# Norms that take their power on a few columns, and low parts of weights made on VectorE, in a hybrid decoder step

## The chip, the cores and the metric

One Trainium2 chip, one core of it. The metric is the device time of one execution in microseconds. Engines in the rows: PE is TensorE (PEld its weight loads), DVE is VectorE, ACT is ScalarE, POOL is GpSimd, SP is the queue that issues the DMAs.

## What is computed

One layer of a decoder trunk for 2048 new positions of a prompt and 64 tokens of running sequences (8 x 8), all in fp32, 1024 columns wide. Half of the mixer is a diagonal state space model (S5), half a gated linear recurrence (HGRN2). Cut to what matters here:

```python
def rmsnorm(x, g):
    r = x * lax.rsqrt(jnp.mean(x * x, axis=-1, keepdims=True) + EPS)
    return r * g

h = rmsnorm(x, norm_mix)
proj = h @ w_in                        # 1024 -> 512 + 4 * 512
y5 = s5_mixer(...)                     # scan, gelu, GLU
yh = hgrn2_mixer(...)                  # chunked recurrence
x = x + jnp.concatenate([y5, yh], -1) @ w_out
h2 = rmsnorm(x, norm_ffn)
x = x + (jax.nn.silu(h2 @ w_gate) * (h2 @ w_up)) @ w_down   # 1024 -> 2816 -> 1024
y = rmsnorm(x, norm_final)
```

## The kernel before

Tokens lie in the free dimension: the 2112 tokens are three blocks of 704 (FT), each two halves of 352 (FH), and the features lie on the 128 partitions. The norms before the FFN and at the end therefore sum over partitions.

**Products.** Every fp32 product is made of three matmuls in the fp32r type: the operand is split into a high part (ScalarE's copy, hi) and a low part (the difference, lo), and hi·hi, hi·lo and lo·hi are added. The output projection, gate and up, and down run by a seven-product scheme for 2 x 2 blocks of the matrices: `w_prep` loads the four quarters of a weight tile into a raw tile (`wr`, two buffers), makes four sums and differences of them on VectorE (L1037, L1038, L1044, L1045), and splits seven operands: ScalarE writes the high part (L1031), GpSimd the low part (L1032). Operands rotate over 7, later 10 buffers (`e.ws`). `x_slots` does the same for the activations, whose low part is VectorE's (L1009).

**A unit.** `seven` interleaves two weight tiles: for each of seven products and each tile 12 matmuls of 352 columns (`nk` = 4, in one group of three `nk` = 3), a set, and after each set a `sink`. Products use three kinds of PSUM bank in the order A Q B A B A A; a later set adds into a bank that an earlier one has left, so it waits for the earlier sink. Sinks are VectorE's sums from PSUM (`acc_sink` L1091, `gate_sink` L1105, `up_sink` L1128) or ScalarE's copies. In gate and up, VectorE also makes the product (L1129, L1119) and four combinations for the down projection (L976 to L979).

**Stages.** First the mixer's own projections and scans, then `mix` for the three blocks (output projection with `w_out`), `combine_y` (combinations of the mixer's output, through DRAM) and `norm2` (the norm before the FFN, its combinations stored to `h_s`); then `ffn` for the three blocks: 11 gate and up units, then for three groups of columns two units of the down projection. `final` of a block is issued after two units of the next block's `ffn`, the last one at the end.

**A norm.** `norm_r` squares on ScalarE, adds up eight tiles on VectorE (`sum`, L1169), sums over partitions with an fp32 matmul by a matrix of ones (L1174), which leaves the same row of 352 sums on all 128 partitions, scales on VectorE (L1175) and takes the power −0.5 on GpSimd for 128 x 704 elements (L1176). VectorE multiplies with the result (`rr_f` in `norm2` at L1185, `rr_z` in `final` at L1201). The norm at the start works otherwise: `inv_rms` (L285) takes the power on a few columns of row sums, `spread` (L293) puts them on a diagonal and spreads it by matmuls.

**Order.** A scheduler sets each engine's order by modelled times; every engine runs its queue in order. Tiles come from pools, a new one waits for the old one's readers.

Of the kernel before, what the change touches and what calls it, by code (L numbers as in the profile page):

```python
# [9 lines left out]
F32 = mybir.dt.float32  # L10
F32R = mybir.dt.float32r
I32 = mybir.dt.int32
AF = mybir.ActivationFunctionType
ALU = mybir.AluOpType
# [4 lines left out]
P = 128  # L19
D = 1024  # L20
# [8 lines left out]
EPS = 1e-6  # L29
# [236 lines left out]
def tiles_of(t0, n):  # L266
    r = []
    while n > 0:
        w = min(P, n)
        r.append((t0, w))  # L270
        t0 += w
        n -= w
    return r


def parts_of(tiles):
    nt = len(tiles)
    full = sum(1 for t in tiles if t[1] == P)
    parts = [(P, 0, full)] if full else []
    if full < nt:  # L280
        parts.append((tiles[-1][1], full, nt))
    return parts


def inv_rms(e, ss, tiles, r, name):  # L285
    nc = e.nc
    st = e.small.tile([P, 4], F32, tag="st", name=f"st_{name}")
    for rows, a, b in parts_of(tiles):
        nc.vector.tensor_scalar(st[:rows, a:b], ss[:rows, a:b], 1.0 / D, EPS, op0=ALU.mult, op1=ALU.add)
        nc.gpsimd.tensor_tensor(r[:rows, a:b], st[:rows, a:b], e.mhalf[:rows, 0:b - a], op=ALU.pow)  # L290


def spread(e, r, tiles, name):  # L293
    nc = e.nc
    dg = e.diag.tile([P, 4, P], F32, tag="dg", name=f"dg_{name}")
    for rows, a, b in parts_of(tiles):
        nc.vector.tensor_tensor(dg[:rows, a:b], e.ident[:rows, None, :].to_broadcast([rows, b - a, P]),
                                r[:rows, a:b, None].to_broadcast([rows, b - a, P]), op=ALU.mult)
    pr = e.ps_x.tile([P, 512], F32, tag="x", name=f"rr_{name}")
    for j, (o, w) in enumerate(tiles):  # L300
        nc.tensor.matmul(pr[:, o:o + w], e.ones[:w], dg[:w, j, :w], start=True, stop=True)
    return pr
# [25 lines left out]
def op_norm(e, t0, n, r, name):  # L328
    nc = e.nc
    pr = spread(e, r, tiles_of(0, n), name)  # L330
    pcs = pieces_of(n)
    op = []
    for j, (k, nk) in enumerate(pcs):
        flat = raw_tile(e, f"x{name}_{j}")[:, :nk * n]
        raw = flat.rearrange("p (k t) -> p k t", t=n)
        nc.sync.dma_start(raw, fm(e.i["xT"], k, nk, t0, n))
        for i in range(nk):
            nc.vector.scalar_tensor_tensor(raw[:, i], raw[:, i], e.gain[:, k + i:k + i + 1], pr[:, :n],
                                           op0=ALU.mult, op1=ALU.mult)
        hi, lo = wtile(e, f"x{name}_{j}", e.ops)  # L340
        split(e, flat, hi[:, :nk * n], lo[:, :nk * n], nc.gpsimd if j % 2 else nc.vector)
        op.append((hi, lo))
    return (t0, n, op_k(op, pcs, n))
# [608 lines left out]
FT = 704  # L952
FH = FT // 2
# [60 lines left out]
def w_prep(e, mats, nk):  # L1014

    nc = e.nc
    n = nk * P
    v = nc.vector
    out = [[] for _ in mats]
    gens = []  # L1020

    def prep(srcs, name, ops):
        raw = e.wraw.tile([P, 6, 512], F32, tag="wr", name=f"wr_{name}")
        for fh in range(2):
            nc.sync.dma_start(raw[:, 2 * fh:2 * fh + 2, :n], srcs[fh].rearrange("p (h f) -> p h f", h=2))
        a11, a12, a21, a22, s1, s2 = (raw[:, i, :n] for i in range(6))

        def sp(src):
            ws = e.ws.pick()
            hi, lo = (ws.tile([P, 512], F32R, tag="w" + c, name=f"w{c}_{name}_{len(ops)}")[:, :n] for c in "hl")  # L1030
            nc.scalar.activation(hi, src, AF.Copy)  # L1031
            nc.gpsimd.tensor_tensor(lo, src, hi.bitcast(F32), op=ALU.subtract)  # L1032
            ops.append((hi, lo))

        sp(a11)
        yield
        v.tensor_tensor(s1, a21, a22, op=ALU.add)  # L1037
        v.tensor_tensor(s2, s1, a11, op=ALU.subtract)  # L1038
        sp(a12)
        yield  # L1040
        sp(s1)
        yield
        sp(s2)
        v.tensor_tensor(a12, a12, s2, op=ALU.subtract)  # L1044
        v.tensor_tensor(a21, a11, a21, op=ALU.subtract)  # L1045
        yield
        sp(a12)
        yield
        sp(a21)
        yield  # L1050
        sp(a22)
        yield

    gens = [prep(srcs, name, ops) for (srcs, name), ops in zip(mats, out)]
    for _ in range(7):
        for g in gens:
            next(g)
    return out
# [98 lines left out]
def norm_r(e, x, name):  # L1157

    nc = e.nc
    tot = None  # L1160
    for j in range(4):
        for d in (j, j + 4):
            if tot is None:
                tot = e.nrm.tile([P, FT], F32, tag="sum", name=f"sum_{name}", bufs=1)
                nc.scalar.activation(tot, x[d], AF.Square)
                continue
            sq = e.nrm.tile([P, FT], F32, tag="sq", name=f"sq_{name}_{d}")
            nc.scalar.activation(sq, x[d], AF.Square)
            nc.vector.tensor_tensor(tot, tot, sq, op=ALU.add)  # L1169
    r = e.nrm.tile([P, FT], F32, tag="sq", name=f"rr_{name}")  # L1170
    for h in range(2):
        hs = slice(h * FH, h * FH + FH)
        ps = e.psN.tile([P, 512], F32, tag="n", name=f"ss_{name}_{h}")[:, :FH]
        nc.tensor.matmul(ps, e.ones, tot[:, hs], start=True, stop=True)  # L1174
        nc.vector.tensor_scalar(r[:, hs], ps, 1.0 / D, EPS, op0=ALU.mult, op1=ALU.add)  # L1175
    nc.gpsimd.tensor_tensor(r, r, e.mhalf[:, 0:1].to_broadcast([P, FT]), op=ALU.pow)  # L1176
    return r


def norm2(e, b, x):  # L1180
    nc = e.nc
    r = norm_r(e, x, f"f{b}")
    for j in range(4):
        for d in (j, j + 4):
            nc.vector.scalar_tensor_tensor(x[d], x[d], e.gain[:, KD + d:KD + d + 1], r, op0=ALU.mult, op1=ALU.mult)  # L1185
        B = [x[d][:, h * FH:h * FH + FH] for d in (j, j + 4) for h in range(2)]
        T = e.mtmp.tile([P, 4, FH], F32, tag="mt", name=f"ht{b}_{j}")
        combine(nc.vector, [T[:, i] for i in range(4)], *B)
        dst = e.h_s[b]
        for slot, t in ((0, B[0]), (1, B[2]), (4, B[3])):  # L1190
            nc.sync.dma_start(dst[:, slot, j], t)
        nc.sync.dma_start(dst[:, 2:4, j], T[:, 0:2])
        nc.sync.dma_start(dst[:, 5:7, j], T[:, 2:4])


def final(e, b, x):
    nc = e.nc
    r = norm_r(e, x, f"z{b}")
    for j in range(4):
        for d in (j, j + 4):  # L1200
            nc.vector.scalar_tensor_tensor(x[d], x[d], e.gain[:, 2 * KD + d:2 * KD + d + 1], r, op0=ALU.mult, op1=ALU.mult)  # L1201
            nc.sync.dma_start(e.o["yT"][d * P:(d + 1) * P, b * FT:(b + 1) * FT], x[d])
# [253 lines left out]
```

## Time and profile before

| what | value |
|---|---|
| median of 3 runs | 3372.87 us (3363.42 to 3374.15) |
| the profiled execution | 3370.24 us, span 3368.5 us |
| mean granted TensorE clock | 0.861 of full |
| GpSimd, six powers of a norm (L1176) | 338.0 + 337.9 us |
| GpSimd, low parts of weights (L1032) | 354.9 + 382.7 + 353.0 + 143.1 us, 798 instructions |

The rows that were read stand further below. In a row of a group, the line number is that of the kernel before; then engine, operation, output<-inputs by the program's names, shape and count; after the bar the busy time in us and the mean of one in ns, then idle time of the engine just before such instructions and what ended most of it. In a timeline, the number in brackets is the idle time before the instruction and what released it. PEclk is the granted TensorE clock as a share of 2.4 GHz.

### The profile page before, as it was taken

What the parts mean: (1) busy time and instruction counts of PE and PEld (TensorE: products, weight loads), DVE (VectorE), ACT (ScalarE), POOL (GpSimd) and SP (SyncE); (2) the same over time, 40 slices, a digit from 0 to 9 for tenths busy, and PEclk for the clock granted to TensorE, in tenths of its full rate; (3) what the DMA queues carried; (4) which work ended last, traced back from release to release, by engine and by line L of the source; (5) the groups of instructions that cost most, each with busy time, mean ns of one, the idle gap of its engine ahead of it and who ended that gap; (6) DMA issues with size and microseconds to landing.
All of it is one profiled execution on the core that took longest, in us unless ns stands there. A gap on an engine that the chain in (4) does not pass through costs nothing.

```text
span 3368.5 us, 44865 instructions
## 1 busy us (share of the span) xinstructions
PE 2398.2 (71%) x16813; PEld 2210.8 (66%) x16813; DVE 2269.8 (67%) x2692; ACT 996.7 (30%) x1848; POOL 2300.7 (68%) x1587
## 2 busy tenths in 40 slices
PE   7989999997713705029999985298998816898840
PEld 6977677785703705029998985288988816898840
DVE  8754545455596896946678788667777795667730
ACT  4322222222301302004434442043434402344310
POOL 4176585511587698866667778976767797666778
PEclk9999999998856857559999998599999957999975
DMA  8865644545414704123324431142353204334300
GB/s 253 226 226 163 182 152 144 161 141 194 162 59 149 258 16 143 57 83 125 138 100 159 142 138 47 68 166 104 138 176 131 99 4 167 114 118 156 131 19 34
DMA packets 249323, 441.57 MB, mean 131 GB/s; under 512 B 80265, under 2 KB 165586, under 8 KB 249106
## 3 DMA queue, kind: packets, MB, share of 16 engines
q1 hardware_dynamic: 249106, 438.71, 39.1%
q8 instruction: 132, 2.16, 0.3%
q14 instruction: 85, 0.70, 0.1%
HBM read 314.86 MB, written 123.76 MB: 130 GB/s over the span
## 4 chain that ended last, share of the span: by engine, by line
PE 30%; DVE 21%; POOL 19%; DMA 12%; issue 10%; POOLq 3%; ACT 2%; SPq 1%; DVEq 0%; ACTq 0%
POOL rr_f L1176 7%; PE pA_u L1076 4%; POOLq L1448 3%; POOL rr_z L1176 3%; PE pA_g L1076 3%; DMA wr_u<-in_w_up_u 3%; PE pA_d L1076 3%; DVE ct L976 2%; DMA wr_wd<-in_w_down_u 2%; POOL wl_wd L1032 2%; PE ps_v L263 2%; PE ps_u L263 2%; DVE s L1129 2%; PE ps_f L263 1%; PE pQ_g L1076 1%
## 5 line engine op out<-in xcount | busy, mean ns | idle before, releaser
L1032 POOL TENSOR_TENSOR wl_u<-wr_u,wh_u 128x512 fp32r<-128x512 f32 x231 | 354.9, 1541 | 198.5 <-ACT wh_u L1031 154.6
L1032 POOL TENSOR_TENSOR wl_wd<-wr_wd,wh_wd 128x512 fp32r<-128x512 f32 (+1 forms) x252 | 382.7, 1545 | 151.9 <-ACT wh_wd L1031 137.8
L1032 POOL TENSOR_TENSOR wl_g<-wr_g,wh_g 128x512 fp32r<-128x512 f32 x231 | 353.0, 1531 | 140.4 <-ACT wh_g L1031 136.2
L1176 POOL TENSOR_TENSOR rr_z<-rr_z,mhalf 128x704 f32<-128x704 f32 x3 | 338.0, 112665 | 18.5 <-DVE rr_z L1175 18.5
L1176 POOL TENSOR_TENSOR rr_f<-rr_f,mhalf 128x704 f32<-128x704 f32 x3 | 337.9, 112625 | 10.9 <-DVE rr_f L1175 10.9
L1076 PE MATMUL pA_g<-xh_h,wh_g 128*128 128x352 f32 x528 | 186.1, 352 | 220.5 <-ACT s L1103 137.2
L1076 PEld LDWEIGHTS pA_g<-xh_h,wh_g 128*128 128x128 f32 x528 | 107.1, 203 | 231.7 <-ACT s L1103 138.1
L1076 PE MATMUL pA_g<-xh_h,wl_g 128*128 128x352 f32 x528 | 182.1, 345 | 98.8 <-POOL wl_g L1032 98.8
L1076 PE MATMUL pA_o<-xh_y,wh_wo 128*128 128x352 f32 x192 | 73.2, 385 | 247.3 <-ACT xh_y L1008 117.3
L1076 PE MATMUL pA_u<-xh_h,wh_u 128*128 128x352 f32 x528 | 178.7, 338 | 85.3 <-ACT u L1126 72.7
L1032 POOL TENSOR_TENSOR wl_wo<-wr_wo,wh_wo 128x512 fp32r<-128x512 f32 x84 | 143.1, 1731 | 109.2 <-ACT wh_wo L1031 100.2
L1076 PE MATMUL pA_d<-xh_s,wh_wd 128*128 128x352 f32 x528 | 179.7, 340 | 44.3 <-DVE acc_d L1091 44.1
L1076 PEld LDWEIGHTS pA_o<-xh_y,wh_wo 128*128 128x128 f32 x192 | 43.3, 227 | 254.3 <-ACT xh_y L1008 118.9
L1031 ACT ACTIVATE wh_wd<-wr_wd 128x512 fp32r<-128x512 f32 (+1 forms) x252 | 140.5, 588 | 221.7 <-DMA wr_wd<-in_w_down_u 97.7
L1129 DVE TENSOR_TENSOR s<-s,u 128x352 f32<-128x352 f32 x99 | 183.0, 1849 | 11.9 <-ACT s L1106 6.1
L1031 ACT ACTIVATE wh_g<-wr_g 128x512 fp32r<-128x512 f32 x231 | 143.1, 624 | 150.9 <-DMA wr_g<-in_w_gate_u 69.8
L1031 ACT ACTIVATE wh_u<-wr_u 128x512 fp32r<-128x512 f32 x231 | 143.0, 625 | 149.7 <-DMA wr_u<-in_w_up_u 47.7
L1076 PE MATMUL pA_g<-xl_h,wh_g 128*128 128x352 f32 x528 | 180.5, 342 | 0.0
L1106 ACT ACTIVATE s<-s 128x352 f32<-128x352 f32 x99 | 49.2, 497 | 431.7 <-DVE s L1105 430.9
L1076 PE MATMUL pA_d<-xh_s,wl_wd 128*128 128x352 f32 x528 | 176.1, 334 | 0.0
L1076 PE MATMUL pA_d<-xl_s,wh_wd 128*128 128x352 f32 x528 | 176.0, 333 | 0.0
L1076 PE MATMUL pA_u<-xh_h,wl_u 128*128 128x352 f32 x528 | 175.2, 332 | 0.5 <-POOL wl_u L1032 0.5
(495 smaller groups left out, 8546.6 us busy)
## 6 DMA issues: line engine op xcount, KB each, us to landing
wr_g<-in_w_gate_u SPq DMA_DIRECT2D x66, 512.0 KB, 4.5
wr_u<-in_w_up_u SPq DMA_DIRECT2D x66, 512.0 KB, 5.8
xr_s<-s_s SPq DMA_DIRECT2D x42, 704.0 KB, 4.3
wr_wd<-in_w_down_u SPq DMA_DIRECT2D x48, 512.0 KB, 5.7
s_s<-T SPq DMA_DIRECT2D x132, 176.0 KB, 1.8
s_s<-s SPq DMA_DIRECT2D x99, 176.0 KB, 1.9
xr_h<-h_s SPq DMA_DIRECT2D x21, 704.0 KB, 4.4
wr_wo<-in_w_out_u SPq DMA_DIRECT2D x24, 512.0 KB, 7.2
```

What stands on the lines that cost most here:

```text
L263: e.nc.tensor.matmul(out, whl[k][a], xhl[k][b], start=start and i == 0, stop=stop and i == len(seq) - 1)
L976: v.tensor_tensor(t[0], b12, b11, op=ALU.subtract)
L1031: nc.scalar.activation(hi, src, AF.Copy)
L1032: nc.gpsimd.tensor_tensor(lo, src, hi.bitcast(F32), op=ALU.subtract)
L1076: nc.tensor.matmul(ps, W[i][w][:, ks], X[i][x][:, k], start=first and k == 0 and c == 0, stop=i in (1, 4, 6) and k == nk - 1 and c == 2, s ...
L1106: nc.scalar.activation(s[w], s[w], AF.Silu)
L1129: v.tensor_tensor(s[w], s[w], u[w], op=ALU.mult)
L1176: nc.gpsimd.tensor_tensor(r, r, e.mhalf[:, 0:1].to_broadcast([P, FT]), op=ALU.pow)
L1448: with tile.TileContext(nc, schedule_with_timeline_sim=True) as tc:
```

## The change

`norm_r` transposes its sums. For each half the sums over partitions come from three matmuls with the sum tile as the stationary operand and one column of ones as the moving one: 352 tokens land on the partitions of three columns (128, 128 and 96 rows). `inv_rms` scales them on VectorE and takes the power on GpSimd, two instructions (128x2 and 96x1) each. A new function, cut out of `spread`, multiplies the identity with them to a diagonal; three matmuls by ones spread it over the partitions; ScalarE copies the result to the tile `r`. All PSUM tiles of this come from the pool `psN` with one buffer. In `w_prep` the low part goes from GpSimd to VectorE. Lines after the new function move by 6, after `norm_r` by 13.

```diff
-def spread(e, r, tiles, name):
+def diagonal(e, r, tiles, name):
     nc = e.nc
     dg = e.diag.tile([P, 4, P], F32, tag="dg", name=f"dg_{name}")
     for rows, a, b in parts_of(tiles):
         nc.vector.tensor_tensor(dg[:rows, a:b], e.ident[:rows, None, :].to_broadcast([rows, b - a, P]),
                                 r[:rows, a:b, None].to_broadcast([rows, b - a, P]), op=ALU.mult)
+    return dg
+
+
+def spread(e, r, tiles, name):
+    nc = e.nc
+    dg = diagonal(e, r, tiles, name)
     pr = e.ps_x.tile([P, 512], F32, tag="x", name=f"rr_{name}")
...
             nc.scalar.activation(hi, src, AF.Copy)
-            nc.gpsimd.tensor_tensor(lo, src, hi.bitcast(F32), op=ALU.subtract)
+            v.tensor_tensor(lo, src, hi.bitcast(F32), op=ALU.subtract)
...
     for h in range(2):
-        hs = slice(h * FH, h * FH + FH)
-        ps = e.psN.tile([P, 512], F32, tag="n", name=f"ss_{name}_{h}")[:, :FH]
-        nc.tensor.matmul(ps, e.ones, tot[:, hs], start=True, stop=True)
-        nc.vector.tensor_scalar(r[:, hs], ps, 1.0 / D, EPS, op0=ALU.mult, op1=ALU.add)
-    nc.gpsimd.tensor_tensor(r, r, e.mhalf[:, 0:1].to_broadcast([P, FT]), op=ALU.pow)
+        o = h * FH
+        tl = tiles_of(0, FH)
+        ss = e.psN.tile([P, 512], F32, tag="n", name=f"ss_{name}_{h}")
+        for j, (c, w) in enumerate(tl):
+            nc.tensor.matmul(ss[:w, j:j + 1], tot[:, o + c:o + c + w], e.ones[:, 0:1], start=True, stop=True)
+        rc = e.small.tile([P, 4], F32, tag="r", name=f"r_{name}_{h}")
+        inv_rms(e, ss, tl, rc, f"{name}_{h}")
+        dg = diagonal(e, rc, tl, f"{name}_{h}")
+        pr = e.psN.tile([P, 512], F32, tag="n", name=f"pr_{name}_{h}")
+        for j, (c, w) in enumerate(tl):
+            nc.tensor.matmul(pr[:, c:c + w], e.ones[:w], dg[:w, j, :w], start=True, stop=True)
+        nc.scalar.activation(r[:, o:o + FH], pr[:, :FH], AF.Copy)
     return r
```

The order that the scheduler makes is the same on all engines up to the first unit of the output projection. Behind it, VectorE's queue in a gate and up unit of the first block (`s_8`, `u_8` and `T_8` are the running unit's tiles, `wr_g`, `wr_u` the next one's raw tiles) reads, before the change:

```order
L1038 TENSOR_TENSOR wr_u_0_13075<-wr_u_0_13075 128x512
L1045 TENSOR_TENSOR wr_u_0_13075<-wr_u_0_13075 128x512
L1105 TENSOR_TENSOR s_8_0_12954<-s_8_0_12954,pB_g_0_12912 128x352
L1044 TENSOR_TENSOR wr_g_0_13068<-wr_g_0_13068 128x512
L1128 TENSOR_TENSOR u_8_0_12968<-u_8_0_12968,pB_u_0_12927 128x352
L1044 TENSOR_TENSOR wr_u_0_13075<-wr_u_0_13075 128x512
L1129 TENSOR_TENSOR s_8_0_12954<-s_8_0_12954,u_8_0_12968 128x352
L976 TENSOR_TENSOR T_8_0_13053<-s_8_0_12954,s_8_0_12865 128x352
L1105 TENSOR_TENSOR s_8_0_12925<-s_8_0_12925,pA_g_0_12852 128x352
```

and at the same place in the changed kernel (`wl_g`, `wl_u` are low parts, L1038; L1111 is the sum that was L1105):

```order
L1038 TENSOR_TENSOR wl_g_0_1_13172<-wr_g_0_13155,wh_g_0_1_13171 128x512
L1038 TENSOR_TENSOR wl_u_0_1_13178<-wr_u_0_13162,wh_u_0_1_13177 128x512
L1043 TENSOR_TENSOR wr_u_0_13162<-wr_u_0_13162 128x512
L1050 TENSOR_TENSOR wr_g_0_13155<-wr_g_0_13155 128x512
L1111 TENSOR_TENSOR s_8_0_13041<-s_8_0_13041,pB_g_0_12999 128x352
L1038 TENSOR_TENSOR wl_g_0_2_13182<-wr_g_0_13155,wh_g_0_2_13181 128x512
L1044 TENSOR_TENSOR wr_u_0_13162<-wr_u_0_13162 128x512
L1051 TENSOR_TENSOR wr_u_0_13162<-wr_u_0_13162 128x512
L1134 TENSOR_TENSOR u_8_0_13055<-u_8_0_13055,pB_u_0_13014 128x352
L1038 TENSOR_TENSOR wl_u_0_2_13186<-wr_u_0_13162,wh_u_0_2_13185 128x512
L1050 TENSOR_TENSOR wr_u_0_13162<-wr_u_0_13162 128x512
L1111 TENSOR_TENSOR s_8_0_13012<-s_8_0_13012,pA_g_0_12939 128x352
```

The sums from PSUM (pB_g, pB_u, pA_g) stand in the same sequence, now with the next unit's low parts between them.

GpSimd's queue at the third block's norm before the FFN (`rr_f`), before:

```order
L1032 TENSOR_TENSOR wl_g_0_0_11928<-wr_g_0_11924,wh_g_0_0_11927 128x512
L1032 TENSOR_TENSOR wl_u_0_0_11935<-wr_u_0_11931,wh_u_0_0_11934 128x512
L1032 TENSOR_TENSOR wl_g_0_1_11941<-wr_g_0_11924,wh_g_0_1_11940 128x512
L1176 TENSOR_TENSOR rr_f_11535<-rr_f_11535,mhalf 128x704
L1032 TENSOR_TENSOR wl_u_0_1_11947<-wr_u_0_11931,wh_u_0_1_11946 128x512
```

and in the changed kernel (`r_f`, `r_z` are the few columns):

```order
L290 TENSOR_TENSOR r_f_0_11598<-st_f_0_11599,mhalf 128x2
L290 TENSOR_TENSOR r_f_0_11598<-st_f_0_11599,mhalf 96x1
L290 TENSOR_TENSOR r_f_1_11616<-st_f_1_11617,mhalf 128x2
L290 TENSOR_TENSOR r_f_1_11616<-st_f_1_11617,mhalf 96x1
L290 TENSOR_TENSOR r_z_0_17119<-st_z_0_17120,mhalf 128x2
```

From the output projection to the end its queue holds nothing but 24 such powers.

VectorE's queue at the end of the program, before:

```order
L1169 TENSOR_TENSOR sum_z_26072<-sum_z_26072,sq_z_3_26089 128x704
L1169 TENSOR_TENSOR sum_z_26072<-sum_z_26072,sq_z_7_26092 128x704
L1175 TENSOR_SCALAR rr_z_26095<-ss_z_0_26096 128x352
L1175 TENSOR_SCALAR rr_z_26095<-ss_z_1_26099 128x352
L1201 SCALAR_TENSOR_TENSOR acc_d_24466<-acc_d_24466,gain,rr_z_26095 128x704
```

and in the changed kernel (`st` are the scaled columns, `dg` the diagonal):

```order
L1175 TENSOR_TENSOR sum_z_26217<-sum_z_26217,sq_z_7_26237 128x704
L289 TENSOR_SCALAR st_z_0_26246<-ss_z_0_26241 128x2
L289 TENSOR_SCALAR st_z_0_26246<-ss_z_0_26241 96x1
L297 TENSOR_TENSOR dg_z_0_26251<-consts,r_z_0_26245 128x256
L297 TENSOR_TENSOR dg_z_0_26251<-consts,r_z_0_26245 96x128
L289 TENSOR_SCALAR st_z_1_26264<-ss_z_1_26259 128x2
L289 TENSOR_SCALAR st_z_1_26264<-ss_z_1_26259 96x1
L297 TENSOR_TENSOR dg_z_1_26269<-consts,r_z_1_26263 128x256
L297 TENSOR_TENSOR dg_z_1_26269<-consts,r_z_1_26263 96x128
L1214 SCALAR_TENSOR_TENSOR acc_d_24611<-acc_d_24611,gain,rr_z_26240 128x704
```

The second half's columns follow the first half's diagonal in the queue, and the eight multiplications follow both.

## Rows read from the trace of the kernel before

**Rows 1.** The page's busy times of the engines, share of the span, instructions

```profile
PE 2398.2 (71%) x16813; PEld 2210.8 (66%) x16813; DVE 2269.8 (67%) x2692; ACT 996.7 (30%) x1848; POOL 2300.7 (68%) x1587
```

**Rows 2.** The page's groups: line, operation, shapes, count, busy us, mean ns, idle

```profile
L1032 POOL TENSOR_TENSOR wl_u<-wr_u,wh_u 128x512 fp32r<-128x512 f32 x231 | 354.9, 1541 | 198.5 <-ACT wh_u L1031 154.6
...
L1176 POOL TENSOR_TENSOR rr_z<-rr_z,mhalf 128x704 f32<-128x704 f32 x3 | 338.0, 112665 | 18.5 <-DVE rr_z L1175 18.5
...
L1129 DVE TENSOR_TENSOR s<-s,u 128x352 f32<-128x352 f32 x99 | 183.0, 1849 | 11.9 <-ACT s L1106 6.1
```

**Rows 3.** VectorE's timeline, beside an idle GpSimd (but 2047.00): the same columns

```profile
1086.26 1.62 DVE L1009 TENSOR_TENSOR xl_y<-xr_y,xh_y 128x1408 fp32r<-128x1408 f32 x1 [1.40 <-ACT xh_y L1008]
1087.80 0.51 DVE L1091 TENSOR_TENSOR acc_m<-acc_m,pB_o 128x352 f32<-128x352 f32 x1
...
2041.79 0.69 DVE L1038 TENSOR_TENSOR wr_g<-wr_g 128x512 f32<-128x512 f32 x1
2042.40 0.69 DVE L1045 TENSOR_TENSOR wr_g<-wr_g 128x512 f32<-128x512 f32 x1
...
2047.00 1.78 DVE L1045 TENSOR_TENSOR wr_u<-wr_u 128x512 f32<-128x512 f32 x1
```

**Rows 4.** Stretch, length; busy us (count) of PE, PEld, DVE, ACT, POOL; PEclk; DMA

```profile
848.00:1505.00 657.00, 230.83 (x1140) 214.93 (x1140) 497.79 (x301) 112.31 (x155) 508.35 (x104) 0.67 0.34 117
950.60:1032.80 82.20, 0.00 (x0) 0.00 (x0) 80.26 (x1) 0.00 (x0) 82.18 (x1) 0.50 0.02 8
1175.70:1288.20 112.50, 13.91 (x68) 13.09 (x67) 84.89 (x14) 7.05 (x12) 112.50 (x2) 0.57 0.07 26
1362.40:1475.40 113.00, 0.00 (x0) 0.00 (x0) 83.42 (x4) 0.00 (x0) 112.95 (x2) 0.51 0.00 0
1505.00:3238.30 1733.30, 1394.01 (x8206) 1366.35 (x8204) 1279.56 (x1219) 637.58 (x1124) 1279.61 (x699) 0.91 0.34 119
2058.00:2171.00 113.00, 20.41 (x112) 19.83 (x110) 85.09 (x8) 6.53 (x14) 113.00 (x3) 0.59 0.02 9
3238.30:3368.50 130.20, 2.40 (x4) 0.80 (x4) 11.14 (x14) 1.46 (x2) 112.47 (x1) 0.52 0.06 22
```

**Rows 5.** VectorE's timeline at the fifth power: start us, duration us, instruction, idle

```profile
2693.25 76.88 DVE L1129 TENSOR_TENSOR s<-s,u 128x352 f32<-128x352 f32 x1
2770.05 0.51 DVE L1105 TENSOR_TENSOR s<-s,pB_g 128x352 f32<-128x352 f32 x1
2770.48 0.51 DVE L1128 TENSOR_TENSOR u<-u,pB_u 128x352 f32<-128x352 f32 x1
...
2800.47 10.20 DVE L1201 SCALAR_TENSOR_TENSOR acc_d<-acc_d,gain,rr_z 128x704 f32<-128x704 f32 x7 [28.27 <-POOL rr_z L1176]
```

**Rows 6.** The chain of work that ended last: start us, us, what

```profile
1507.90 1.91 PE pA_g L1076 x12
...
1632.73 3.89 PE pA_g L1076 x12
...
1848.06 4.09 PE pA_d L1076 x24
```

**Rows 7.** TensorE's waits, 1540 to 1800 us: us in total, times, longest us

```profile
PE pA_g L1076 <- DVE s L1105: 20.1, 9, 3.7
```

**Rows 8.** TensorE's timeline, two restarts after a stall, idle time in brackets

```profile
1632.73 0.66 PE L1076 MATMUL pA_g<-xh_h,wh_g 128*128 128x352 f32 x1 [3.69 <-DVE s L1105]
...
1848.06 0.43 PE L1076 MATMUL pA_d<-xh_s,wh_wd 128*128 128x352 f32 x1 [1.13 <-DVE acc_d L1091]
```

**Rows 9.** One line's instructions: ns min/median/max, first and last start, forms

```profile
L290 POOL TENSOR_TENSOR rcol<-st_u,mhalf x7: 592/724/1037, 11.5 to 80.8; 128x2 f32<-128x2 f32 x4, 128x4 f32<-128x4 f32 x2, 64x1 f32<-64x1 f32 x1
...
L301 PE MATMUL rr_u<-dg_u,ones x34: 271/275/582, 12.7 to 107.0; 128*128 128x128 f32 x32, 64*128 64x64 f32 x2
```

**Rows 10.** VectorE's timeline at the end

```profile
3357.94 6.99 DVE L1201 SCALAR_TENSOR_TENSOR acc_d<-acc_d,gain,rr_z 128x704 f32<-128x704 f32 x8 [112.65 <-POOL rr_z L1176]
```

**Rows 11.** The page's DMA issues: count, KB each, median us to landing

```profile
wr_g<-in_w_gate_u SPq DMA_DIRECT2D x66, 512.0 KB, 4.5
```

## The prediction

> **What bounds the kernel now.** I read the page's busy times first: no engine is the bound of the whole. TensorE, VectorE and GpSimd are each busy about 70% of the span [rows 1], so the limits change from stage to stage. The costliest groups show where GpSimd's time goes: six powers over 704 columns at 112.7 us each (three named rr_z, three alike named rr_f), and 798 low parts at about 1.54 us [rows 2]. In the same rows VectorE's multiplication of two 352-column SBUF tiles (L1129) takes 1849 ns on average, while one of 512 columns takes 690 ns beside an idle GpSimd [rows 3]. GpSimd holds VectorE up.
>
> The table by stretch [rows 4] then says what that costs. The changed lines are not at work before 848 us. From 848 to 1505 us (mixer's output projection, its combination and the second norm) TensorE is busy 231 of 657 us. In the three stretches that lie under a power there, it issues 0, 68 and 0 matmuls. From 1505 to 3238 us (FFN) it issues 8206, and in the stretch under the fourth power only 112 of them. The last 130 us hold four matmuls.
>
> Why a power stops everything is seen in VectorE's timeline around the fifth one [rows 5]: a multiplication that should take less than 0.69 us takes 76.88 us, the next ones run at once, and then the queue stands 28 us more for rr_z itself. TensorE starves, since its sums are taken off PSUM by that queue.
>
> Between the powers the FFN runs at 1733.3 − 113 − 112.8 = 1507.5 us for 8206 − 2 × 112 = 7982 matmuls (the fifth power's stretch counted like the fourth's), 0.189 us each. At full clock a set of 12 takes 1.91 us, 0.159 each [rows 6]. What is lost is one stall in nearly every unit: in 260 us TensorE waits nine times, 20.1 us in all, for the same instruction, L1105 of VectorE [rows 7], the sum that must leave bank A before the last set may start; and after a stall of 3.69 us the next set takes 3.89 instead of 1.91 us, at the lower of the two clocks (1.2 instead of 2.4 GHz) [rows 6, 8].
>
> **The change part by part.** *The powers.* Six instructions over 704 columns go. In their place are 24 over one or two columns: 0.72 us each, median of the few such ones that the kernel already has [rows 9]. A half of a norm becomes a chain: single-column sums (three matmuls, taken as the diagonal's, 3 × 0.275), two scalings (2 × 0.52 at most, which is what 352 columns cost), two powers (1.45), the diagonal (two VectorE instructions over as many columns, 2 × 0.52), three matmuls (0.83), ScalarE's copy (taken as one scaling, 0.52): 5.7 us, with hand-overs 6. The two halves follow each other, since the PSUM pool has one buffer: 12 us a norm. Bounds: 4 us a half if they overlap with the queue, 10 if each hand-over costs a microsecond.
>
> *Where the time under a power goes.* First norm: VectorE frozen for 82.2 us; the chain of loads and combinations behind it simply starts earlier, and 6 us remain. Second: 112.5 us in which 68 matmuls ran (11 us); with the new chain partly beside them, 20 remain. Third: 113 us in which nothing ran; 12 remain, since TensorE's queue has the new matmuls in a row with the FFN behind them. What is late next there are the single-buffered combinations and stores after it (the 30 us before 1505), which stay. Fourth and fifth: 113 + 112.8 us with 224 matmuls (36 us); 45 remain, since the order leaves far more than 12 us of matmuls between a half's sums and its spread. Sixth: nothing hides it. After the last matmul 130.2 us become 3 (last sums) + 12 + 7.0 (eight gains) + 4 (the last store) = 26 [rows 4, 10].
>
> *The low parts.* 798 instructions leave GpSimd for VectorE. Their price there is that of the same kind beside idle GpSimd: starts lie 0.61 us apart at 128x512, against 1.78 us for the same instruction beside a GpSimd one [rows 3]. A 1408-column low part takes 1.55 us to the next start [rows 3], a 352-column sum 0.43 [rows 5]. So a gate-and-up unit costs VectorE 8 combinations and 14 low parts, 22 × 0.61 = 13.4, and 14 sums and products, 14 × 0.43 = 6.0: 19.4 us beside TensorE's 14 × 1.91 = 26.7. A pass of the down projection costs 7 × 1.55 + 2 × 19.4 = 49.7 beside 2 × 26.7 = 53.4. VectorE fits, with a quarter to spare in the first and with 7% in the second.
>
> *The wait that is added.* A low part waits for ScalarE's high part, and that for a weight buffer which TensorE frees. On GpSimd this held up nothing else; on VectorE the sums of PSUM queue behind it, and TensorE waits for those. I follow one unit. The last of 14 operands gets its buffer (there are ten) when TensorE ends the fourth set, 7.7 us into the unit; about 9 us in, the raw tile is free; the next one lands 4.5 us after its issue [rows 11], at 14. In the order, 16 VectorE instructions stand from the first low part on that tile to the sum of bank A, some 9 us, one of which waits until TensorE's ninth set at 17.3. That puts the sum at 23.9 us, where the last set could start at 23.1: 1 us of stall in place of 2.2, and after 1.13 us of idle time the next 24 matmuls took 4.09 us, so the clock holds there [rows 6, 8]. I take 26.7 + 1.0 + 0.8 for what I cannot see = 28.5 us a unit, 0.170 a matmul. In the down passes, with 7% to spare, I take 60 us for 53.4, 0.178. The bounds: 0.163 (no stall worth naming) and 0.200 (worse than now by the share that VectorE lacks).
>
> *Sum.* Before 848 us the order of every engine is the same: 848. The 349 us of the mixer's part that lie under no power become 340: the contended instructions get faster, 84 low parts come to the queue (51 us, much of it in waits for transfers). FFN: two thirds of 7982 matmuls at 0.1696 and one third at 0.178 give 1376. 848 + 340 + 6 + 20 + 12 + 1376 + 45 + 26 = 2673 us of span, against 3368.5. The profiled execution took 1.7 us more than its span, the median 2.6 more than that: 2677.
>
> **The rivals.** *TensorE becomes the bound*: every sum in time, 0.163 a matmul, 1301 us, and 315 in the mixer's part: 2560 with all else equal or a little less. For it speaks the quarter that VectorE has to spare in the units; against it the down passes.
>
> *VectorE's queue becomes the bound*: the FFN keeps its 0.189 or falls to 0.200, 1508 to 1596 us: 2810 to 2900. For it: 93% of a pass, and a queue in which any late tile delays the sums. Against it: VectorE is now slower than that through contention, and TensorE still does 0.189.
>
> *The clock keeps falling*: each unit keeps a stall long enough that the next set runs at 1.2 GHz, 2 to 3 us lost 47 times (7982 / 168), 95 to 140 us: about 2795. The stall of 3.69 us speaks for it, that of 1.13 against [rows 6, 8]. The Trainium skill, page "TensorE: Matmul & The Clock Gate", section "A second HAM failure mode: psum-queue depth-cycling", tells of a kernel where frequent short idles around PSUM banks made the clock swing between its two levels; by that rule this rival is the forecast and the time some 2795; the trace agrees for the long stalls only.
>
> *Slower than before*: the three engines fall into step, so that a set waits for ScalarE's high part (0.6), VectorE's low part (0.7) and a hand-over before each 1.91, some 3.4 us. The FFN's 665 sets would take 2260 us and the kernel about 3560. It decides from 0.26 us a matmul on. Against it: ten weight buffers stand between the engines, and no row shows TensorE waiting for each operand.
>
> *The change doesn't do what it says*, if a power had a fixed price of many microseconds whatever its columns; the 0.72 us [rows 9] speak against it.
>
> **How the numbers follow.** Forecast 58% (2610 to 2760), TensorE bound 12%, VectorE bound 17%, clock 10%, slower 2%, powers still long 1%. The range 2560 to 2830 takes in the forecast, nearly all of the clock's case, about half of each bound's; some 16% stay outside. About 0.3% is what a measurement of this kernel can tell from no change: faster 0.97, within it 0.01, slower 0.02.
>
> **What would show it.** In the profile after: no GpSimd group of the powers or low parts in its list; VectorE's L1129 below 0.69 us and low parts near 0.6 to 0.7; no stretch of 80 us in which one VectorE instruction lasts; the last matmul of the FFN about 26 us before the end; between 848 us and the FFN's steady part some 380 us; in the FFN a unit every 28 to 29 us with stalls near 1 us behind VectorE, and a granted clock above the 0.91 of now [rows 4]. The forecast is wrong if TensorE's waits in the FFN are as long as now but named after low parts, or if the mixer's part keeps more than 450 us.

## The result and the profile after

The changed kernel takes 2540.1 us, median of 4 runs (2523.75 to 2541.89), against 3368.1 for the kernel before (median of 4 runs, one more than in the table ahead): ratio 0.753 (0.750 to 0.757). The forecast was 2677 us with a range from 2560 to 2830. The direction and the large steps came as forecast; the time lies 20 us below the range. The profiled execution after took 2539.93 us with a span of 2538.1.

The page's busy line after the change, in the form of [rows 1]: TensorE (PE) from 71% to 91%, GpSimd (POOL) from 68% to 17%. VectorE (DVE) is busy for 1865 instead of 2270 us, although it has taken over 798 instructions.

```profile
PE 2316.8 (91%) x16933; PEld 2162.3 (85%) x16933; DVE 1865.3 (73%) x3526; ACT 1010.5 (40%) x1860; POOL 421.7 (17%) x807
```

Two of its groups, the power over few columns (24 such instructions, 12 of them in this row, stand for the six over 704) and a low part where it is now (columns as in [rows 2]):

```profile
L290 POOL TENSOR_TENSOR r_z<-st_z,mhalf 128x2 f32<-128x2 f32 (+1 forms) x12 | 12.8, 1081 | 1358.2 <-DVE st_z L289 1358.2
L1038 DVE TENSOR_TENSOR wl_u<-wr_u,wh_u 128x512 fp32r<-128x512 f32 x231 | 158.1, 686 | 40.9 <-ACT wh_u L1037 34.3
```

and, from the list of groups by line, the product that was L1129:

```profile
L1135 DVE TENSOR_TENSOR s<-s,u 128x352 f32<-128x352 f32 x99 | 51.3, 518 | 4.4 <-ACT s L1112 3.8
```

Twelve powers of 1.08 us stand where three of 112.7 stood [rows 2]; a low part costs 0.69 us instead of 1.54, and the product 0.52 instead of 1.85.

For the stretches one mark is needed that both traces have: ScalarE's copy `u` right before the FFN runs without a break. It starts at 1505.2 us before and at 1186.6 us after. The table by stretch, after, in the order mixer's part, FFN, tail (columns as in [rows 4], the share and rate of the DMA behind the clock):

```profile
848.00:1186.60 338.60, 213.90 (x1200) 204.93 (x1200) 259.54 (x425) 115.63 (x161) 9.77 (x12) 0.81 0.67 231
1186.60:2514.40 1327.80, 1323.17 (x8244) 1319.12 (x8244) 1115.43 (x1928) 647.91 (x1127) 10.38 (x8) 1.00 0.45 155
2514.40:2538.10 23.70, 5.32 (x25) 4.65 (x24) 11.96 (x20) 2.50 (x5) 2.44 (x4) 0.59 0.32 122
```

| stretch | before | forecast | after | off by |
|---|---|---|---|---|
| up to 848 us | 848 | 848 | 848 | 0 |
| mixer's part (340 + 6 + 20 + 12) | 657.2 | 378 | 338.6 | -39 |
| FFN (1376 + 45) | 1733.1 | 1421 | 1327.8 | -93 |
| tail | 130.2 | 26 | 23.7 | -2 |

In the FFN TensorE is now busy for 1323 of 1328 us at the full granted clock (1.00, before 0.91). Its waits in the FFN are few; these are all that are listed (columns as in [rows 7]); the nine waits for the sum of bank A that took 20 us in 260 [rows 7] are gone.

```profile
PE pB_u L1082 <- ACT u L1132: 2.0, 1, 2.0
PE pQ_g L1082 <- ACT wh_g L1037: 1.3, 2, 1.0
PE pA_d L1082 <- DVE acc_d L1097: 1.2, 2, 1.0
PE pA_u L1082 <- DVE wl_u L1038: 1.0, 2, 0.6
PE pA_g L1082 <- DVE acc_d L1097: 0.4, 1, 0.4
```

So what came is the first rival of the prediction: TensorE is the bound of the FFN, at 0.161 us a matmul (1327.8 us for 8244).

### The profile page after: what moved, and what is told of

Same layout as the page of the kernel before. It is cut to its first block, busy times and chain, and to the rows that moved or that the text cites. A ratio compares the mean times of both kernels' runs of the same rounds, so it can differ in the third digit from the quotient of the medians.

```text
span 2538.1 us, 44181 instructions
## 1 busy us (share of the span) xinstructions
PE 2316.8 (91%) x16933; PEld 2162.3 (85%) x16933; DVE 1865.3 (73%) x3526; ACT 1010.5 (40%) x1860; POOL 421.7 (17%) x807
## 4 chain that ended last, share of the span: by engine, by line
PE 65%; DVE 13%; DMA 9%; POOL 7%; issue 2%; SPq 2%; ACT 2%; DVEq 0%; ACTq 0%; POOLq 0%
PE pA_g L1082 10%; PE pA_u L1082 10%; PE pA_d L1082 8%; PE pB_u L1082 5%; PE pB_g L1082 5%; PE pB_d L1082 4%; PE ps_u L263 2%; PE pQ_g L1082 2%; PE pQ_u L1082 2%; PE ps_v L263 2%; PE pQ_d L1082 2%; PE pz L263 2%; PE ps_g L263 2%; DMA cy<-y_s 1%; PE ps_q L263 1%
## 5 line engine op out<-in xcount | busy, mean ns | idle before, releaser
L290 POOL TENSOR_TENSOR r_z<-st_z,mhalf 128x2 f32<-128x2 f32 (+1 forms) x12 | 12.8, 1081 | 1358.2 <-DVE st_z L289 1358.2
L1038 DVE TENSOR_TENSOR wl_g<-wr_g,wh_g 128x512 fp32r<-128x512 f32 x231 | 158.0, 686 | 92.4 <-ACT wh_g L1037 92.3
L1037 ACT ACTIVATE wh_wd<-wr_wd 128x512 fp32r<-128x512 f32 (+1 forms) x252 | 140.2, 589 | 193.7 <-DMA wr_wd<-in_w_down_u 70.2
L1082 PE MATMUL pA_g<-xh_h,wh_g 128*128 128x352 f32 x528 | 173.2, 328 | 26.5 <-ACT s L1109 21.8
L1038 DVE TENSOR_TENSOR wl_u<-wr_u,wh_u 128x512 fp32r<-128x512 f32 x231 | 158.1, 686 | 40.9 <-ACT wh_u L1037 34.3
L1082 PE MATMUL pA_g<-xh_h,wl_g 128*128 128x352 f32 x528 | 171.9, 326 | 0.9 <-DVE wl_g L1038 0.9
L1082 PE MATMUL pA_u<-xl_h,wh_u 128*128 128x352 f32 x528 | 169.4, 321 | 0.0
L1038 DVE TENSOR_TENSOR wl_wd<-wr_wd,wh_wd 128x512 fp32r<-128x512 f32 (+1 forms) x252 | 156.2, 639 | 13.5 <-ACT wh_wd L1037 13.5
L504 DVE TENSOR_TENSOR q<-q,tot 128x256 f32<-128x256 f32 (+1 forms) x96 | 51.2, 533 | 96.9 <-PE p L477 36.5
L1082 PEld LDWEIGHTS pA_g<-xh_h,wl_g 128*128 128x128 f32 x528 | 100.6, 191 | 1.5 <-DVE wl_g L1038 1.5
L1082 PEld LDWEIGHTS pA_g<-xl_h,wh_g 128*128 128x128 f32 x528 | 101.2, 192 | 0.0
```

The source lines that it names most:

```text
L504: vec.tensor_tensor(qv[:, :, 1], qv[:, :, 1], t[:, :, 0:1].to_broadcast(shp), op=ALU.mult)
L1038: v.tensor_tensor(lo, src, hi.bitcast(F32), op=ALU.subtract)
L1082: nc.tensor.matmul(ps, W[i][w][:, ks], X[i][x][:, k], start=first and k == 0 and c == 0, stop=i in (1, 4, 6) and k == nk - 1 and c == 2, s ...
```

## Experiments

**One part at a time.** The first kernel has the changed norms and leaves the low parts on GpSimd (its edit is against the changed kernel); the second has the low parts on VectorE and the old norms (its edit, further down, is against the kernel before).

```diff
-            v.tensor_tensor(lo, src, hi.bitcast(F32), op=ALU.subtract)
+            nc.gpsimd.tensor_tensor(lo, src, hi.bitcast(F32), op=ALU.subtract)
```

> The changed norms alone, low parts left on GpSimd. Theory (the two parts act in different stretches and add up): the six stretches of the powers shrink as in the changed kernel and the FFN between them keeps 0.189 us a matmul; 3368 - 555 = some 2815 us (2780 to 2850), L1129's counterpart still near 1.8 us, TensorE still waiting some 2 us a unit for the same sum of bank A. Rival (the powers leave a backlog that is the cause of the stalls between them): FFN at 0.165 or below and 2640 or less.

Measured: 2764 us (2743 to 2769), ratio 0.819 (0.815 to 0.823), 51 us below the 2815 and 16 below the range that was expected. The FFN kept its slow pace. Its stretch by the same mark (1217.3 to 2742.9 us) and TensorE's main waits between 1240 and 2740 us:

```profile
1217.30:2742.90 1525.60, 1385.86 (x8244) 1363.53 (x8244) 1128.30 (x1231) 639.96 (x1128) 1061.27 (x705) 0.96 0.39 135
```

```profile
PE pA_g L1082 <- DVE s L1111: 70.9, 31, 5.2
PE pA_d L1082 <- DVE acc_d L1097: 45.4, 26, 4.3
```

1525.6 us for 8244 matmuls are 0.185 each, against 0.189 forecast, and 31 units wait 2.3 us each for the sum of bank A. The rival (0.165 or below) falls: the stalls are not a backlog of the powers, they belong to the low parts on GpSimd. What was expected of the product that was L1129, still near 1.8 us, did not come: it took 1.06 (see "A mean that misled").

```diff
-            nc.gpsimd.tensor_tensor(lo, src, hi.bitcast(F32), op=ALU.subtract)
+            v.tensor_tensor(lo, src, hi.bitcast(F32), op=ALU.subtract)
```

> The low parts on VectorE alone, six powers over 704 columns as before. Theory: FFN between the powers at 0.160 us a matmul (1277 instead of 1508 us), some 25 less in the mixer's part, powers still 113 us each: 3368 - 231 - 25 = some 3110 us (3070 to 3150), and the two experiments' gains sum to the whole change's 828. Rival (a power freezes VectorE only because GpSimd's low parts wait behind it): the stretches of the powers shrink here too, and the time falls below 3000.

Measured: 3097 us (3093 to 3105), ratio 0.919 (0.916 to 0.922). The six powers last about as long as before (113.6 and 114.9 us in the mean). Its FFN by the same mark, and TensorE's waits in it (1495 to 2972 us), which show one pair of long ones, one for each of the two powers that lie there, and next to nothing else:

```profile
1494.30:2972.40 1478.10, 1324.23 (x8204) 1318.77 (x8204) 1274.56 (x1916) 643.07 (x1124) 232.09 (x2) 0.95 0.40 139
```

```profile
PE pB_u L1076 <- ACT u L1126: 75.6, 2, 74.6
PE pB_u L1076 <- DVE wl_u L1032: 71.1, 1, 71.1
PE pA_g L1076 <- ACT s L1103: 3.3, 1, 3.3
```

The powers' stretches stay, so the rival falls and the theory holds in kind, but the gains of the two kernels do not simply add as it said: 604 + 272 = 876 against 828. By stretches (from the spans), the FFN loses 207.5 us by the norms alone, 255.0 by the low parts alone and 405.3 by both. Most of the 57 us that are counted twice are told by the trace of before: there TensorE waits for low parts that stand behind a power in GpSimd's queue. Of its waits between 1505 and 3238 us, the long ones read:

```profile
PE pA_g L1076 <- POOL wl_g L1032: 98.0, 3, 97.0
...
PE pA_u L1076 <- ACT u L1126: 72.7, 3, 70.2
...
PE pB_g L1076 <- POOL wl_g L1032: 23.4, 1, 23.4
```

The second and the third belong to the fourth power, the first to the fifth: 70.2 + 23.4 + 97.0 = 190.6 us, against 74.6 + 71.1 = 145.7 with the low parts on VectorE. That is 45 of the 57; the other 12 are not traced.

A power in the FFN therefore cost (1733.1 - 1525.6) / 2 = 104 us where GpSimd had the low parts, and (1478.1 - 1327.8) / 2 = 75 us where it had nothing else. Either part of the change shortens that.

**What a power is priced by.** The kernel before, with the power on 32 of 128 partitions; the other 96 are left without it.

```diff
-    nc.gpsimd.tensor_tensor(r, r, e.mhalf[:, 0:1].to_broadcast([P, FT]), op=ALU.pow)
+    nc.gpsimd.tensor_tensor(r[:32], r[:32], e.mhalf[:32, 0:1].to_broadcast([32, FT]), op=ALU.pow)
```

> The kernel before with its six powers on 32 of the 128 partitions, 704 columns as before; the other 96 partitions are left without the power. Theory (the price goes by columns): 112.7 us each as before, and 3368 us. Rival (it goes by elements): 28 us each, and some 400 to 500 us less, the transposition not needed for the gain.

Measured, in a single run: 3365.9 us against 3368.6. The theory holds. Its row:

```profile
L1176 POOL TENSOR_TENSOR rr_z<-rr_z,mhalf 32x704 f32<-32x704 f32 x3 | 338.0, 112654 | 18.4 <-DVE rr_z L1175 18.4
```

112.65 us on 32 partitions, 112.67 on 128 [rows 2]: the price does not follow the partitions. It goes by columns, 0.160 us each over 704 of them. Putting the tokens on the partitions is what makes the power cheap; fewer rows of the old form would have brought nothing.

**How much room VectorE has.** The changed kernel with low parts made twice on VectorE, in gate and up (14 a unit) or in gate alone (7 a unit).

```diff
             v.tensor_tensor(lo, src, hi.bitcast(F32), op=ALU.subtract)
+            if name[0] == "g" or name[0] == "u":
+                v.tensor_tensor(lo, src, hi.bitcast(F32), op=ALU.subtract)
```

> The changed kernel with every low part of gate and up made twice on VectorE, 14 more instructions of 0.60 us a unit: 19.4 + 8.4 = 27.8 us for VectorE beside 26.9 for TensorE. Theory (VectorE has a reserve of a quarter in these units, and only beyond it TensorE waits): a unit of 28 to 29 us, 33 units by 1 to 2 us, 2575 to 2610 us. Rival (the blind working: each low part ahead of bank A's sum makes TensorE wait by as much): the sum comes 5 us later, at least 3 us of stall in each unit beside a falling clock, 2650 or more.

Measured: 2700 us (2695 to 2703), ratio 0.801 (0.799 to 0.804). The size is the rival's, the reason is not. TensorE's longest waits between 1210 and 2680 us:

```profile
PE pB_g L1084 <- DVE wl_g L1040: 17.9, 11, 5.8
PE pB_u L1084 <- ACT wh_u L1037: 17.1, 13, 4.0
PE pB_u L1084 <- DVE wl_u L1040: 12.1, 12, 1.8
PE pA_u L1084 <- DVE wl_u L1040: 11.3, 11, 3.7
```

They name the weights' parts, not the sum of bank A. The order had changed as well: sets are broken into runs of two matmuls. VectorE's work was more than the 27.8 us that were worked out: in three stretches of gate and up units it is busy for 277.5 of 300, 292.5 of 310 and 295.4 of 320 us (1200 to 1500, 1700 to 2010, 2200 to 2520), 28.1 to 29.4 us for the 168 matmuls of a unit. That is 1.2 to 2.5 us above TensorE's 26.9. The FFN as a whole (1195.4 to 2676.2 us) grew by 153 us: TensorE stands 94 us of it, where it stood 5, and its matmuls take 64 us longer at a granted clock of 0.97. Why a unit costs 4.8 us and not 1.2 to 2.5 is not settled by this.

```diff
             v.tensor_tensor(lo, src, hi.bitcast(F32), op=ALU.subtract)
+            if name[0] == "g":
+                v.tensor_tensor(lo, src, hi.bitcast(F32), op=ALU.subtract)
```

> The changed kernel with each low part of the gate weights made twice, 7 more instructions of 0.60 us a unit: 19.4 + 4.2 = 23.6 us for VectorE beside 26.9 for TensorE (88%). The 14 of the run before cost 159 us, 4.8 a unit, where 27.8 us of VectorE's work alone would have made it 0.9 to 2. Theory (the sum of bank A comes a median of 2.6 us ahead of its need; up to that, more work in the queue costs nothing): 2540 to 2560 us. Rival (the queue costs what stands ahead of the sum, whatever the reserve): half the cost of 14, some 80 us, 2620.

Measured: 2557 us (2554 to 2560), ratio 0.759 (0.757 to 0.760): 17 us for 231 more instructions (139 us of VectorE's time). The time lies in the range of the theory, though the cost is not nothing: at 88% of TensorE's time the queue costs half a microsecond a unit, at 103% by the expectation's own sum nearly five.

**When the raw tile comes free.** The changed kernel with 8 buffers for split weights.

```diff
-    px2, pw2, pq2 = pool("xs2", 1), pool("ws2", 3), pool("xr2", 1)
+    px2, pw2, pq2 = pool("xs2", 1), pool("ws2", 1), pool("xr2", 1)
...
-    e.ws.set((pw, 7), (pw2, 3))
+    e.ws.set((pw, 7), (pw2, 1))
```

> The changed kernel with 8 instead of 10 buffers for split weights. Theory (what sets the sum of bank A is when the raw tile comes free, and that goes by the operand buffers): two operands later, 3.9 us, against a median slack of 2.6 us: about 1 us of stall in most of the 47 units' worth and some lower clock, 2575 to 2640 us. Rival (the two raw tiles set it, or TensorE's order moves the need as far back): within 10 us of the changed kernel.

Measured: 2548 us (2547 to 2548), ratio 0.756 (0.755 to 0.757), not to be told from the changed kernel's 0.753 (0.750 to 0.757). The theory falls, the rival holds, and the order shows how: between gate's sixth set (which the sum of bank A takes off PSUM) and its last set there now lie 36.3 matmuls instead of 32.5 in the mean over the 33 units, so the need moved back by 0.6 us, and the sum itself came only 0.6 us later (also in the mean).

**Half of the low parts on GpSimd.**

```diff
-            v.tensor_tensor(lo, src, hi.bitcast(F32), op=ALU.subtract)
+            (nc.gpsimd if name[0] == "u" else v).tensor_tensor(lo, src, hi.bitcast(F32), op=ALU.subtract)
```

> The changed kernel with the low parts of the up weights back on GpSimd, those of gate and of the down projection on VectorE: GpSimd works 7 x 1.54 = 10.8 of a unit's 26.9 us, and the order gives the sum of bank A 27 matmuls (4.3 us) in the mean before it is needed, instead of 32. Theory A (the sum came late before because GpSimd, 21.6 us a unit, frees the raw tile late; at half that it keeps pace): no stalls, 2535 to 2560 us. Theory B (each VectorE instruction that reads two SBUF tiles beside a GpSimd one takes about twice to three times as long, and those queue ahead of the sum, at any load): half of the 225 us that all low parts on GpSimd cost, 2620 to 2680 us.

Measured: 2580 us (2578 to 2584), ratio 0.766 (0.764 to 0.768): some 40 us more than the changed kernel, between the two theories. Contention is there at half the load. Two groups of this kernel show it side by side, the same first sum of a raw tile, once mostly beside GpSimd's work and once not:

```profile
L1043 DVE TENSOR_TENSOR wr_u<-wr_u 128x512 f32<-128x512 f32 x33 | 48.5, 1469 | 11.7 <-DMA wr_u<-in_w_up_u 11.6
...
L1043 DVE TENSOR_TENSOR wr_g<-wr_g 128x512 f32<-128x512 f32 x33 | 22.7, 688 | 6.8 <-DMA wr_g<-in_w_gate_u 6.4
```

and the waits for the sum of bank A return (1200 to 2540 us):

```profile
PE pA_g L1082 <- DVE s L1111: 17.1, 11, 3.4
```

But 40 us are a fifth, not half, of the 198 by which all low parts on GpSimd lengthen the FFN (1525.6 against 1327.8). GpSimd is not short of time here: in the first block's gate and up units (1200 to 1455 us) it is busy for 95 of 255 us. The sum comes later than in the changed kernel, and the order also leaves it fewer matmuls before its need (27 instead of 32.5, table below); the two were not separated. How much of the rest of the 198 us is contention at the full load and how much is GpSimd's own pace stays open.

**What is left in the mixer's part.** The changed kernel with one more raw buffer for activations.

```diff
-    px, pw, pr, pq = pool("xs", 7), pool("ws", 7), pool("wr", 2), pool("xr", 1)
+    px, pw, pr, pq = pool("xs", 7), pool("ws", 7), pool("wr", 2), pool("xr", 2)
...
-    e.xraw.set((pq, 1), (pq2, 1))
+    e.xraw.set((pq, 2), (pq2, 1))
```

> The changed kernel with one more buffer for the raw tiles of activations (two instead of one during the first block's output projection, three instead of two from then on). Theory (the mixer's part is held by that ring: load 4 to 7 us, high part 1.4, low part 1.6, next load; 150 of its 352 us TensorE stands): 30 to 60 us less, 2480 to 2510 us. Rival (VectorE's queue and the stores hold it, 270 of 352 us busy): 2530 to 2540 us.

Measured: 2507 us (2504 to 2512), ratio 0.7442 (0.7425 to 0.7459), below the changed kernel's 0.7531 (0.7495 to 0.7567): the theory holds, near the upper end of its range. In the changed kernel TensorE's longest wait of the mixer's part (848 to 1186.6 us) was for this ring, the high part of a new activation tile:

```profile
PE pA_o L1082 <- ACT xh_y L1014: 39.6, 3, 37.5
```

With three buffers it is gone, and the longest ones there (848 to 1147.9 us) are

```profile
PE pA_g L1082 <- ACT s L1109: 21.7, 1, 21.7
PE pA_o L1082 <- ACT wh_wo L1037: 21.6, 2, 21.3
PE pA_o L1082 <- DVE acc_m L1097: 19.3, 5, 15.6
```

The part takes 299.9 instead of 338.6 us. The next step brought nothing:

```diff
     def tile(self, shape, dt, tag, name):
+        if name[:2] == "ct":
+            return self.e.mtmp.tile(shape, dt, tag="mt", name=name)
         return self.e.xraw.tile(shape, dt, tag="xr", name=name)
```

> The kernel with three raw buffers, and the results of the mixer's combinations of blocks 1 and 2 in the tile that norm2 uses later, so that they take no raw buffer. Theory (combinations hold two raw buffers each for a load, 2.4 us of work and a store): another 10 to 30 us less than with three raw buffers alone, 2460 to 2490 us. Rival (that single tile becomes the new serial chain): the same or up to 15 us more than with three raw buffers alone.

Measured: 2513 us (2510 to 2517), ratio 0.7456 (0.7442 to 0.7471): the rival, no gain.

**The tail.** The kernel with three raw buffers, and for the last norm's second half a PSUM pool of its own.

```diff
-    final(e, FB - 1, got[FB - 1]["x"])
+    final(e, FB - 1, got[FB - 1]["x"], [(e.psN, "n"), (pQ2, "q2")])
```

(`norm_r` takes both PSUM tiles of half h from the h-th of these pools.)

> The kernel with three raw buffers, and for the last norm a PSUM pool of its own for each half, so that the second half's sums do not wait for the first half's copy. Theory: the chain of the two halves overlaps, 9.6 us become some 6, and the tail 20 instead of 23.9: 2503 us (2500 to 2507). Rival (the two halves' instructions queue on VectorE and GpSimd anyway): 2507 as with three raw buffers alone; the difference is near what can be measured.

Measured: 2502 us (2500 to 2510), ratio 0.7434 (0.7411 to 0.7456). Against three raw buffers alone no difference can be claimed from the times; the trace shows the step. In the changed kernel TensorE's last instructions form two chains, one behind the other:

```profile
2518.01 0.75 PE L1182 MATMUL ss_z<-ones,sum_z 128*128 128x1 f32 x6 [3.50 <-DVE sum_z L1175]
2520.40 1.57 PE L1188 MATMUL pr_z<-dg_z,ones 128*128 128x128 f32 x6 [1.65 <-DVE dg_z L297]
2522.52 1.33 PE L1182 MATMUL ss_z<-ones,sum_z 128*128 128x1 f32 x6 [0.55 <-ACT rr_z L1189]
2525.49 1.57 PE L1188 MATMUL pr_z<-dg_z,ones 128*128 128x128 f32 x6 [1.64 <-DVE dg_z L297]
```

and here both halves' sums run in a row:

```profile
2480.45 2.47 PE L1183 MATMUL ss_z<-ones,sum_z 128*128 128x1 f32 x12 [3.50 <-DVE sum_z L1175]
2483.40 1.57 PE L1189 MATMUL pr_z<-dg_z,ones 128*128 128x128 f32 x6 [0.48 <-DVE st_z L289]
2485.55 1.60 PE L1189 MATMUL pr_z<-dg_z,ones 128*128 128x128 f32 x6 [0.59 <-DVE dg_z L297]
```

From the first sums to the gains it is 7.2 us instead of 9.6 (2487.68 - 2480.45, 2527.60 - 2518.01). This kernel, at 2502 us, has the lowest median here.

## Where the prediction was right and where it failed

**The powers: right, but for the mixer's part.** The price of the small power (0.72 us a piece forecast; one pair of 128x2 and 96x1 takes 1.22 us in the tail; in the FFN, beside VectorE's work, it is 1.30 us a piece, 10.38 us for 8, and TensorE waits for none of them), the half of a norm (6 us forecast, 4.5 and 5.1 measured in the tail), the tail (26, measured 23.7) and the 45 us for the fourth and fifth norm fit: 1327.8 us less 7982 matmuls at 0.160 leave 51 for those two stretches, worked out and not measured by itself (0.160 is the pace of the first block's gate and up, 1907 matmuls in the 305 us from 1200 to 1505). Of the three stretches in the mixer's part the norms alone leave 20 us (1217.3 - 848 - 349.5, if the time under no power stays as it was), where 6 + 20 + 12 = 38 stood: too much; that most of the chain lies beside other work there is a reading, no run shows it by itself.

**The low parts on VectorE: price right, wait wrong.** The 0.61 us between starts holds, and so does the load: in the first block's down projection VectorE is busy for 91% (forecast 93%).

```profile
1462.00:1600.00 138.00, 137.92 (x862) 137.51 (x861) 125.55 (x215) 63.30 (x97) 0.00 (x0) 1.00 0.48 162
```

TensorE is busy for 137.92 of these 138 us. The step that failed is the one after it: "I take 26.7 + 1.0 + 0.8 for what I cannot see" and "60 us for 53.4". Neither the stall nor the surcharges came, and they make the FFN's miss: 7982 matmuls at 0.160 are 1277 us, not 1376, and a unit of 168 takes 26.9 us, not 28.5. A load of 91 or 93% was read as a reason for stalls; it was none. The bound had the same fault: "0.163 (no stall worth naming)" adds 0.004 without a reason to the 0.159 of its own row [rows 6], and the measured pace lies below it.

The microsecond of stall rested on two times within a unit: the sum of bank A done at 23.9 us, the last set able to start at 23.1. Both were off. The unit that begins some 1306.1 us into the trace after (gate's sixth set ends some 19.2 us into a unit in the prediction, 23.1 less two sets of 1.91; its last matmul starts at 1325.14) shows it. First SP's queue, then ScalarE, then VectorE:

```profile
1311.32 0.81 SPq L1031 DMA_DIRECT2D wr_g<-in_w_gate_u  x2
1313.19 0.80 SPq L1031 DMA_DIRECT2D wr_u<-in_w_up_u  x2
```

```profile
1314.93 0.63 ACT L1037 ACTIVATE wh_g<-wr_g 128x512 fp32r<-128x512 f32 x1 [0.56 <-DMA wr_g<-in_w_gate_u]
...
1319.45 0.63 ACT L1037 ACTIVATE wh_u<-wr_u 128x512 fp32r<-128x512 f32 x1 [3.14 <-DMA wr_u<-in_w_up_u]
```

```profile
1320.11 0.69 DVE L1038 TENSOR_TENSOR wl_u<-wr_u,wh_u 128x512 fp32r<-128x512 f32 x1 [1.72 <-ACT wh_u L1037]
...
1327.43 0.52 DVE L1111 TENSOR_TENSOR s<-s,pA_g 128x352 f32<-128x352 f32 x1
```

The raw tiles are asked for 5.2 and 7.1 us into the unit, not at 9, and are there at 8.8 and 13.3; the sum runs at 21.3. And the last set comes later than 23.1, here at 23.5 (1329.65), since the scheduler put more of the next unit's matmuls ahead of it: 27 in this unit and 32.5 in the mean, where the order of before had 25. The changed order could be read ahead of the run; the prediction counted two sets. All 33 units, worked out from the queue orders and from TensorE's and VectorE's timelines (the matmuls between gate's sixth and its last set in the mean; the times as medians, in us from the start of the sixth set's last matmul; free is the time from the sum's end to the last set's start):

| kernel | matmuls between | sum starts | last set starts | free |
|---|---|---|---|---|
| before | 25.0 | 5.96 | 6.53 | 0.05 |
| norms alone | 26.2 | 5.94 | 6.50 | 0.06 |
| up on GpSimd | 26.9 | 3.69 | 4.66 | 0.06 |
| after | 32.5 | 2.29 | 5.15 | 2.61 |
| 8 buffers | 36.3 | 2.86 | 6.24 | 2.78 |
| 7 more low parts | 33.1 | 1.72 | 5.62 | 3.19 |
| 14 more low parts | 20.1 | 1.06 | 2.79 | 0.91 |

A free time near 0.05 is a TensorE that waits for the sum. In the changed kernel no unit has less than 0.73 us free. Most of it is VectorE's: even with 25 matmuls between (4.0 us) the sum, ended 2.8 us after its set's last matmul starts, would be in time in the median. The rest is the order's, which follows the sum when it is modelled later (8 buffers).

**The mixer's part: 39 us too long.** 18 of them are the norms (above). The rest is the low parts: with the new norms they bring 30.7 us there (1217.3 to 1186.6), not the 9 of 349 to 340; without the new norms they bring 10.9 (1505.2 to 1494.3). So the powers had covered most of that gain.

**The rivals.** "TensorE becomes the bound" got 12% and came; against it stood only the down passes' 93%. Its price was wrong as well: by its own terms it is 2677 - (1376 - 1301) - (340 - 315) = 2577 us, inside the range, and not 2560. Against those terms the FFN's pace saved 24 us more (1277 instead of 1301), and the mixer's part with its norms 14 (338.6 instead of 315 + 38). So that TensorE is the bound does not by itself put the time outside the range; the paces did. "VectorE's queue becomes the bound" did not come at 91 to 93%; with 14 more instructions a unit VectorE is busy for 92 to 94% of a unit that has grown longer, and TensorE waits. "The clock keeps falling" did not come: with no stalls the granted clock stayed at 1.00. The lock step is nowhere to be seen in the changed kernel, which lists 5.9 us of waits in the whole FFN.

**A mean that misled.** That VectorE's product (L1129) took 1849 ns on average [rows 2] was read as the price of contention. One of its 99 instructions is the frozen one of 76.88 us [rows 5]; without it the mean is (183.0 - 76.88) / 98 = 1.08 us, and with the norms alone changed it is 1.06, still twice the 0.52 of the changed kernel:

```profile
L1135 DVE TENSOR_TENSOR s<-s,u 128x352 f32<-128x352 f32 x99 | 105.3, 1064 | 9.0 <-ACT s L1112 3.4
```

## What to carry to other kernels

Price an operation by what its time follows (here the columns) before you move or split it; a transposition by a few small matmuls took a power from 112.7 us to two pairs of 1.2 in the tail. An engine that is busy for 90% of the bound's time need not slow the bound: here VectorE at 91% cost TensorE nothing in the down projection, and at 88% half a microsecond a unit in gate and up. What decides is whether its results come ahead of their need: work out that free time for one unit from the changed order, both the moment the result comes and the moment it is needed, and add no surcharge for "what I cannot see" on top of it. Work that shares GpSimd's queue with a long instruction pays for that instruction too, so two changes that each shorten it do not add up.

## What the runs showed of the hardware

A power on GpSimd holds VectorE for less than its own time. The fifth one, before:

```profile
2687.67 112.77 POOL L1176 TENSOR_TENSOR rr_z<-rr_z,mhalf 128x704 f32<-128x704 f32 x1
```

It ends at 2800.44, and the VectorE instruction that waits for its result starts at 2800.47 [rows 5], but the frozen instruction [rows 5] ends at 2693.25 + 76.88 = 2770.13, 30.3 us earlier. In the other four powers of that trace that freeze an instruction it is 30.1 to 30.3 us as well, and the same on 32 partitions, GpSimd's row first and VectorE's behind it (the power ends at 1063.20, the frozen instruction at 1032.90):

```profile
950.73 112.47 POOL L1176 TENSOR_TENSOR rr_f<-rr_f,mhalf 32x704 f32<-32x704 f32 x1 [7.26 <-DVE rr_f L1175]
```

```profile
952.35 80.55 DVE L976 TENSOR_TENSOR ct<-cy 128x352 f32<-128x352 f32 x1 [1.70 <-DMA cy<-y_s]
```

The Trainium skill, page "SBUF — State Buffer", says in its section "Who interferes with whom" that a VectorE instruction with two SBUF inputs contends with a GpSimd instruction that reads SBUF, and in its section "Summary: rules for kernel authors" that the second of the two to issue is blocked until the first finishes. That the later one is blocked, the traces show; that it lasts until the other finishes, these powers do not: the last 30 of 112 us are free for VectorE. Why that is so, no run here tells.
